# W_out scaled and split early, both parts kept in DRAM, and brought into x^T's place by transfers alone

## The chip, the cores and the metric

The kernel runs on one core of one Trainium2 chip. A core has TensorE (PE, with its weight loads shown as PEld), VectorE (DVE), ScalarE (ACT), GpSimd (POOL) and SyncE (SP), which issues all transfers of this kernel. The metric is the device time of one execution in microseconds (us); a kernel's time is the median over its runs. A profile shows one execution.

## The reference

One layer of a streaming encoder, for 1024 prompt tokens and 64 sample tokens with a past of 512, width 1024. All is fp32.

```python
q_f, k_f, v_f, log_f, u_g, v_g, q_s, k_s, v_s = in_proj(x, w_in, b_f)
o_f = fox attention, 6 heads of 64: softmax(q k^T / 8 + c_t - c_s), c = cumsum(log_f), causal
o_s = stick-breaking attention, 6 heads of 64: sigmoid(z_ts) * prod_{s<j<t} (1 - sigmoid(z_tj))
o_g = gelu(u_g) * (tril(W_s) layer_norm(gelu(v_g)) + b_s)   in chunks of 128, 4 groups of 64
o   = per-head rms_norm(concat(o_f, o_g, o_s)) * g_mix
x   = layer_norm(ALPHA * x + o @ w_out)
x   = layer_norm(ALPHA * x + square(relu(x @ w_up)) @ w_down)
```

The outputs are x for both groups of tokens and the new rows of k, v, log_f and of the normalised v of the gating group.

## The kernel before

**Products.** Every fp32 operand of a matmul is split into a high part and a low part (the rest), and a product is three matmuls: high by high, high by low, low by high. So a weight is loaded, copied to the high part on ACT (L331 and others), and the low part is a subtraction on DVE or POOL (helper `lo_sub`, L97).

**Tokens.** There are nine token tiles: eight of 128 prompt tokens and one of 64 sample tokens. `xT` (L301) holds x transposed, two tiles for the upper and lower 512 rows, each with the high and the low parts of all tokens.

**The first stage** is two streams that the program interleaves by hand (the loop from L1077). `fill()` (L931) makes the projections: for each of six head pairs (three fox, then three stick-breaking) k and v for the nine token tiles, three steps for each tile (`kv_stage`), and q in four parts of three steps (`q_stage`); then the gating v (`sgu_v`) behind the fifth pair, the gating u (`sgu_u`) last, and the first two tiles of the mixing (`mix`, MIXED = 2). `attn()` (L979) makes the attention: for every pair, blocks of 256 queries and two heads (`Unit`), then the sample (`Sample`). The loop takes a step of `attn` when its planned cost is behind that of `fill`; `n_f` counts the steps of `fill`. A new block of queries waits until its q is projected and six further steps of `fill` have passed. The order in which instructions then stand on each engine is made by a scheduler that lists them by a planned time; `in_order` (L100) pins a group of them to the order in which they are written.

A stick-breaking block goes from the scores on PE to the mask on DVE (L561), two sigmoids on ACT (L536, L537), a scan on DVE (L538), a product on POOL (L540), transposes on PE (L602), the split on ACT and DVE (L570, L97), and the product with v on PE (L612 to L615).

**W_out.** The rows of W_out are scaled by `g_mix`, and it takes the place of `xT`, since x^T isn't needed once u is projected. `sgu_u` makes two passes over the nine token tiles, first with the upper 512 rows of x^T and then with the lower ones. After a tile of a pass it issues the pieces of W_out that fit in columns already read (`load_wo`, L964): a piece is 128 rows by 512 columns, loaded into a buffer (tags `vp` or `raw`), scaled and rounded to the high part on ACT (L973), and its low part is made on DVE (L974). There are 16 pieces:

```python
due = [(g, 0, t - 4)] if 4 <= t < 8 else [(0, 1, t)] if g == 1 and t < 4 else []
due += [(1, 1, k) for k in range(4)] if g == 1 and t == NB else []
```

**The mixing** (`mix`, L220) takes token tiles in the order `ORD`. `prep` loads the o rows of a tile (L181) and the gating u (L177), multiplies, and normalises per head (L183 to L192); `o_trans` transposes and splits them (L200, L202, L97), and two groups of 24 matmuls (L244), one for each half of the columns, take W_out as the moving operand; a layer norm follows. The second sub-layer comes after this stage; it is not touched.

Of the kernel before, what the change touches and what calls it, by code (L numbers as in the profile page):

```python
# [12 lines left out]
F32 = mybir.dt.float32  # L13
F32R = mybir.dt.float32r
AF = mybir.ActivationFunctionType
ALU = mybir.AluOpType
# [4 lines left out]
P = 128  # L21
PASSES = ((0, 0), (0, 1), (1, 0))
D = 1024
KT = D // P
# [3 lines left out]
NB = TP // P  # L28
# [28 lines left out]
def _build(nc, tc, a, es):  # L57
# [5 lines left out]
    dr = es.enter_context(tc.tile_pool(name="dr", bufs=1, space=DRAM))  # L63
# [27 lines left out]
    h4_dr = dr.tile([NP, 2, P, 4, 2 * P], F32, name="h4_dr")  # L91
    h3_dr = dr.tile([NP, 2, P, 3, 2 * P], F32, name="h3_dr")
    hs_dr = dr.tile([NP, P, 4, 32], F32, name="hs_dr")
    c_dr = dr.tile([6, TP + PAST + TS], F32, name="c_dr")

    def lo_sub(eng, out, src, hi):
# [2 lines left out]
    @contextmanager  # L99
    def in_order(prev=None):  # L100

        traced = nc.cur_bb.bb.instructions
        last = traced[-1]
        yield
        at = next(k for k in reversed(range(len(traced))) if traced[k] is last) + 1
        prev = {} if prev is None else prev
        for i in traced[at:]:
            p = prev.get(i.engine)
            if p is not None:
                tc.add_manual_dep(i, p.name, mybir.DependencyInfo(  # L110
                    mybir.DependencyClass.NoSync, mybir.DependencyReason.DATA), reason="in_order")
            prev[i.engine] = i

    def dma_r(out, in_):
        nc.sync.dma_start(out.bitcast(F32), in_.bitcast(F32))
# [4 lines left out]
    wo = []  # L120
# [147 lines left out]

    MIXED = 2
    written = set()  # L270
    WOC = 0.5

    def ready(t):
        return ("sb2", min(t // 2, 4)) in written
# [8 lines left out]
    with ExitStack() as p1:  # L283
# [484 lines left out]
            return w  # L768

        def sgu_v(wv):  # L770
            wst = sa.tile([P, 4, 2, P], F32R, name="wst")
            wsr = sp.tile([P, 4, P], F32, name="wsr", tag="row", bufs=ROWS)
            nc.sync.dma_start(wsr, a["w_s"].rearrange("l g i j -> i (l g) j"))
            for g in range(4):
# [39 lines left out]
            for t in range(NT):  # L814
                n = trows(t)
                q = t % 4
# [22 lines left out]

        def sgu_u(wu):  # L840
            part = {}
            nc.sync.dma_start(gmx, a["g_mix"].rearrange("l (k p) -> p (l k)", p=P))
            wo.extend([x[:, :, 0:TP], x[:, :, LO:LO + TP]] for x in xT)
            for g in range(2):
                for t in range(NT):
                    n = trows(t)
                    acc = ps.tile([P, 512], F32, name=f"sgu{t}_{g}", tag="acc", bufs=2)
                    yield from tok_mm(acc, 0, wu, t, 0, 256, range(4 * g, 4 * g + 4))
                    if g == 0:
                        if t % 2 == 0:  # L850
                            part[t // 2] = sa.tile([P, 512], F32, name=f"up{t}", tag="kp", bufs=10)
                        r = part[t // 2][:, (t % 2) * 256:(t % 2) * 256 + 256]
                        nc.scalar.activation(r[0:n], acc[0:n, 0:256], AF.Copy)
                    else:
                        r = part[t // 2][:, (t % 2) * 256:(t % 2) * 256 + 256]
                        nc.vector.tensor_tensor(r[0:n], r[0:n], acc[0:n, 0:256], op=ALU.add)
                    if t == NB:
                        fold(nc.vector, r[0:n], acc, 0, 256)
                    if g == 1:
                        u = sp.tile([P, 256], F32, name=f"sguu{t}", tag="gl", bufs=3)  # L860
                        gelu(u[0:n], r[0:n], n, 256, f"u{t}", nc.gpsimd)
                        nc.sync.dma_start(u_dr[t * P:t * P + n, :], u[0:n])
                        if t == 4:
                            mix_open()
                            preps(2, sa)
                    due = [(g, 0, t - 4)] if 4 <= t < 8 else [(0, 1, t)] if g == 1 and t < 4 else []
                    due += [(1, 1, k) for k in range(4)] if g == 1 and t == NB else []
                    for x in due:
                        load_wo(*x)
                    yield 0.109 * 8  # L870

        pairs = []
# [88 lines left out]
            while live["kp"] > 4:  # L961
                yield None

        def load_wo(i, half, q):  # L964

            k = 4 * i + q
            cs = slice(half * 512, (half + 1) * 512)
            raw = (sa.tile([P, 512], F32, name=f"rwo{k}_{half}", tag="vp", bufs=10) if (2 * k + half) % 3
                   else sp.tile([P, 512], F32, name=f"rwo{k}_{half}", tag="raw", bufs=2))
            nc.sync.dma_start(raw, w_out[:, k, cs])  # L970
            hi = wo[i][0][:, q, cs]
            g = gmx[:, k:k + 1]
            nc.scalar.activation(hi, raw, AF.Copy, scale=g)  # L973
            nc.vector.scalar_tensor_tensor(wo[i][1][:, q, cs], raw, g, hi.bitcast(F32),  # L974
                                           op0=ALU.mult, op1=ALU.subtract)

        cur = {"j": 0}

# [84 lines left out]
            xrs[t] = x_load(t)  # L1063
        load_q(pairs[0])
        x_next = [5, 6, 7, 8]
        F, A = fill(), attn()
        next(A)
        cost = {"f": 0.0, "a": 0.0, "f0": None}
# [8 lines left out]
        while f_live or a_live:  # L1077
            if a_live and pend is None:
                go_a = not f_live or (cost["f0"] is not None
                                      and cost["a"] <= cost["f"] - cost["f0"])  # L1080
            elif a_live:
                if pend in done:
                    lead += 1
                go_a = pend in done and (lead > LEAD or not f_live)
            else:
                go_a = False
            if force_a:
                go_a, force_a = True, False
            if go_a:
                if pend is not None:  # L1090
                    if cost["f0"] is None or pend[1] == 0:
                        cost["f0"], cost["a"] = cost["f"], 0.0
                    pend = None
                    lead = 0
                try:
                    c = next(A)
                    if isinstance(c, tuple):
                        pend = c
                        lead = LEAD if c in seen else 0
                        seen.add(c)  # L1100
                    else:
                        cost["a"] += c * RATIO[cur["j"]]
                except StopIteration:
                    a_live = False
            elif f_live:
                try:
                    c = next(F)
                    if c is None:
                        assert a_live and (pend is None or pend in done), "stuck"
                        force_a = True  # L1110
                        continue
                    cost["f"] += c
                    n_f += 1
                    if x_next and n_f % 3 == 0:
                        xrs[x_next[0]] = x_load(x_next[0])
                        x_next.pop(0)
                except StopIteration:
                    f_live = False
                    while later:
                        flush()  # L1120
# [987 lines left out]
```

## Time and profile before

| | us |
|---|---|
| median of 3 runs | 1408.93 |
| lowest and highest run | 1406.53, 1409.12 |
| the profiled execution, time | 1403.64 |
| the profiled execution, span from first to last instruction | 1401.8 |
| mean granted clock of PE | 0.984 |

The profiled execution is not one of the three runs: its own time lies 5.3 us below their median. The span is what the rows below divide; a granted clock of 1 is the full clock of PE.

### The profile page before, as it was taken

What the parts mean: (1) busy time and instruction counts of PE and PEld (TensorE: products, weight loads), DVE (VectorE), ACT (ScalarE), POOL (GpSimd) and SP (SyncE); (2) the same over time, 40 slices, a digit from 0 to 9 for tenths busy, and PEclk for the clock granted to TensorE, in tenths of its full rate; (3) what the DMA queues carried; (4) which work ended last, traced back from release to release, by engine and by line L of the source; (5) the groups of instructions that cost most, each with busy time, mean ns of one, the idle gap of its engine ahead of it and who ended that gap; (6) DMA issues with size and microseconds to landing.
All of it is one profiled execution on the core that took longest, in us unless ns stands there. A gap on an engine that the chain in (4) does not pass through costs nothing.

```text
span 1401.8 us, 24289 instructions
## 1 busy us (share of the span) xinstructions
PE 1323.6 (94%) x8827; PEld 1205.5 (86%) x8827; DVE 996.3 (71%) x1795; ACT 720.1 (51%) x1561; POOL 608.5 (43%) x667
## 2 busy tenths in 40 slices
PE   7899999999989997999899999999998999999996
PEld 6899999999888986866789999999986788887874
DVE  3566566677787499787776677687668677667677
ACT  3366565666565476333432332322256677667665
POOL 3222232356565445755421222122156765555647
PEclk9999999999999998999999999999999999999998
DMA  7334242321313434432223444443468244344343
GB/s 219 72 84 113 58 113 66 83 59 49 95 27 80 115 97 130 143 112 68 76 85 113 160 152 131 153 141 127 162 223 316 90 169 138 130 153 146 106 135 128
DMA packets 150257, 168.87 MB, mean 120 GB/s; under 512 B 27116, under 2 KB 116524, under 8 KB 150136
## 3 DMA queue, kind: packets, MB, share of 16 engines
q1 hardware_dynamic: 150136, 167.30, 38.1%
q8 instruction: 70, 1.15, 0.3%
q14 instruction: 51, 0.42, 0.1%
HBM read 109.26 MB, written 51.71 MB: 115 GB/s over the span
## 4 chain that ended last, share of the span: by engine, by line
PE 54%; DVE 13%; DMA 10%; POOL 8%; ACT 8%; issue 5%; SPq 1%; DVEq 0%; ACTq 0%; POOLq 0%
PE zA L1272 9%; PE zD L1272 6%; PE mx L244 5%; PE kvsb L355 5%; PE kvfox L355 4%; POOL wd L97 3%; DMA rd<-w_down 3%; PE zC L1272 3%; PE zB L1272 3%; DMA awa<-h_dr 2%; POOL rd L1404 2%; PE qfox L496 2%; PE Sfox L554 2%; ACT wd L1212 2%; PE ptfox L602 1%
## 5 line engine op out<-in xcount | busy, mean ns | idle before, releaser
L97 POOL TENSOR_TENSOR wa<-wr,wa 128x512 fp32r<-128x512 f32 x42 | 63.6, 1544 | 225.3 <-ACT wa L1212 203.8
L97 POOL TENSOR_TENSOR wd<-rd,wd 128x512 fp32r<-128x512 f32 x77 | 100.5, 1317 | 108.0 <-ACT wd L1212 94.8
L244 PE MATMUL mx<-xT,oTb 128*128 128x512 f32 (+1 forms) x416 | 105.6, 405 | 1.6 <-ACT oTb L202 1.5
L1272 PE MATMUL zD<-xo,ws 128*128 128x288 f32 (+1 forms) x720 | 98.1, 289 | 3.1 <-DVE h4a L1436 2.7
L1272 PE MATMUL zA<-xo,ws 128*128 128x288 f32 (+1 forms) x720 | 98.2, 290 | 0.0
L1272 PEld LDWEIGHTS zD<-xo,ws 128*128 128x128 f32 x720 | 93.7, 189 | 3.6 <-DVE h4a L1436 2.9
L244 PEld LDWEIGHTS mx<-xT,oTb 128*128 128x128 f32 (+1 forms) x416 | 76.3, 189 | 21.1 <-ACT oTb L202 2.5
L1272 PEld LDWEIGHTS zA<-xo,ws 128*128 128x128 f32 x720 | 94.3, 190 | 0.0
L355 PE MATMUL kvfox<-wkvfox,xT 128*128 128x256 f32 (+3 forms) x624 | 90.8, 294 | 2.4 <-DVE fx L458 1.3
L540 POOL TENSOR_TENSOR sgsb<-sgsb,snsb 128x127 f32<-128x127 f32 (+7 forms) x48 | 58.9, 1228 | 78.7 <-DVE snsb L538 64.3
L1404 POOL TENSOR_TENSOR rd<-rd 128x512 f32<-128x512 f32 x56 | 79.4, 1419 | 30.4 <-DVE b L97 28.1
L355 PE MATMUL kvsb<-wkvsb,xT 128*128 128x256 f32 (+1 forms) x624 | 87.7, 286 | 0.0
L1212 ACT ACTIVATE wd<-rd 128x512 fp32r<-128x512 f32 x105 | 63.4, 623 | 44.2 <-POOL rd L1404 21.9
L1730 PE MATMUL A<-wd,wd 128*128 128x512 f32 x312 | 83.3, 396 | 3.0 <-DVE acc L1697 2.0
L355 PEld LDWEIGHTS kvfox<-wkvfox,xT 128*128 128x128 f32 (+1 forms) x624 | 81.9, 194 | 4.1 <-DVE fx L458 1.6
L538 DVE TENSOR_TENSOR_SCAN snsb<-snsb,one 128x128 f32<-128x128 f32 (+7 forms) x48 | 72.3, 1509 | 13.3 <-ACT snsb L537 12.7
L355 PEld LDWEIGHTS kvsb<-wkvsb,xT 128*128 128x128 f32 (+1 forms) x624 | 79.3, 187 | 0.2
L1283 ACT ACTIVATE sn<-zA 128x256 f32<-128x256 f32 (+1 forms) x80 | 31.0, 390 | 92.2 <-PE zA L1272 77.5
L1730 PEld LDWEIGHTS A<-wd,wd 128*128 128x128 f32 x312 | 58.0, 188 | 19.1 <-DVE acc L1697 3.5
L1730 PE MATMUL A<-wd,h4a 128*128 128x512 f32 x240 | 64.2, 393 | 1.2 <-DVE acc L1697 0.7
L1490 ACT ACTIVATE ws<-wr 128x1024 fp32r<-128x1024 f32 x28 | 29.0, 1057 | 56.9 <-DVE wr L1222 56.9
L1730 PEld LDWEIGHTS A<-wd,h4a 128*128 128x128 f32 x240 | 44.8, 188 | 12.3 <-ACT wd L1212 1.1
(548 smaller groups left out, 3750.5 us busy)
## 6 DMA issues: line engine op xcount, KB each, us to landing
h_dr<-hh SPq DMA_DIRECT2D x30, 512.0 KB, 3.2
rd<-w_down SPq DMA_DIRECT2D x30, 512.0 KB, 4.4
wr<-w_up SPq DMA_DIRECT2D x13, 1024.0 KB, 5.5
hr<-h_dr SPq DMA_DIRECT2D x31, 384.0 KB, 3.8
h_dr<-hh SPq DMA_DIRECT2D x30, 384.0 KB, 4.0
raw<-w_in SPq DMA_DIRECT2D x44, 256.0 KB, 3.4
hx<-h_dr SPq DMA_DIRECT2D x15, 512.0 KB, 3.8
awa<-h_dr SPq DMA_DIRECT2D x15, 512.0 KB, 4.1
```

The source lines that it names most:

```text
L97: eng.tensor_tensor(out, src, hi.bitcast(F32), op=ALU.subtract)
L244: nc.tensor.matmul(acc[0:m], oT[:, k, hx, 0:m], wo[k // 4][hw][:, k % 4, cs], start=(i == 0), stop=(i == len(seq) - 1))
L355: nc.tensor.matmul(acc[0:n, c0:c0 + n1 - n0], xT[k // 4][:, k % 4, c:c + n], wt[:, k, hw, n0:n1], start=(i == 0), stop=(i == len(seq) - 1))
L496: nc.tensor.matmul(acc[:, 0:w], wq[:, k, hw, :], xT[k // 4][:, k % 4, c:c + w], start=(i == 0), stop=(i == len(seq) - 1))
L538: nc.vector.tensor_tensor_scan(g[:, 0:n][:, ::-1], g[:, 0:n][:, ::-1], one.broadcast_to([P, n]), 1.0, op0=ALU.mult, op1=ALU.bypass)
L540: nc.gpsimd.tensor_tensor(s[:, 0:n - 1], s[:, 0:n - 1], g[:, 1:n], op=ALU.mult)
L1212: nc.scalar.activation(hi, raw, AF.Copy)
L1272: nc.tensor.matmul(z, w[:, hw, k], xop(s, bo, hx)[:, k, :], start=(new and k == 0 and j == 0), stop=(k == 3 and j == 2), skip_group_check= ...
L1283: nc.scalar.activation(c, z, AF.Copy)
L1404: eng.tensor_tensor(r[:, o], r[:, x], r[:, y], op=ALU.subtract)
L1490: nc.scalar.activation(ws[:, 0, q, c], src[:, q], AF.Copy)
L1730: nc.tensor.matmul(z, h[:, hx, q, o], wset[self.c % 2][q][:, hw, wb], start=((n in (0, 3) or n == 1 and self.c == 0) and q == 0 and j == 0 ...
```

## The change

W_out is scaled and split while the fox pairs run. `scale_wo` is a generator of three steps for each of the 16 pieces: load the piece, scale and split it on ACT and DVE, and store both parts into `wo_dr` in DRAM. The loop takes a step of it on every second step of `fill`, from the 32nd on. Its instructions are put behind all those that are already written on their engines (`behind`). Its buffers are two that were there, shared by tag: `sq` of the mixing's squares, and `wst` of the gating weights. In `sgu_u`, `load_wo` now issues only transfers, two of 1 MB (high and low part) at each of four places: after token tiles 3 and 8 of either pass. The load of `g_mix` moves from `sgu_u` to the start of `scale_wo`.

```diff
+    wo_dr = dr.tile([2, 2, 2, P, 4, 512], F32, name="wo_dr")
...
+    def behind():
+
+        return in_order({i.engine: i for i in nc.cur_bb.bb.instructions})
...
-    WOC = 0.5
+    WO_FROM, WO_EVERY = 30, 2
...
-            wst = sa.tile([P, 4, 2, P], F32R, name="wst")
+            wst = sa.tile([P, 4, 2, P], F32R, name="wst", tag="wst", bufs=1)
...
-            nc.sync.dma_start(gmx, a["g_mix"].rearrange("l (k p) -> p (l k)", p=P))
...
-                    due = [(g, 0, t - 4)] if 4 <= t < 8 else [(0, 1, t)] if g == 1 and t < 4 else []
-                    due += [(1, 1, k) for k in range(4)] if g == 1 and t == NB else []
-                    for x in due:
-                        load_wo(*x)
+                    if t in (3, NB):
+                        load_wo(g, t // NB)
...
-        def load_wo(i, half, q):
-
-            k = 4 * i + q
-            cs = slice(half * 512, (half + 1) * 512)
-            raw = (sa.tile([P, 512], F32, name=f"rwo{k}_{half}", tag="vp", bufs=10) if (2 * k + half) % 3
-                   else sp.tile([P, 512], F32, name=f"rwo{k}_{half}", tag="raw", bufs=2))
-            nc.sync.dma_start(raw, w_out[:, k, cs])
-            hi = wo[i][0][:, q, cs]
-            g = gmx[:, k:k + 1]
-            nc.scalar.activation(hi, raw, AF.Copy, scale=g)
-            nc.vector.scalar_tensor_tensor(wo[i][1][:, q, cs], raw, g, hi.bitcast(F32),
-                                           op0=ALU.mult, op1=ALU.subtract)
+        def scale_wo():
+
+            nc.sync.dma_start(gmx, a["g_mix"].rearrange("l (k p) -> p (l k)", p=P))
+            for k in range(KT):
+                for half in range(2):
+                    raw = sa.tile([P, 512], F32, name=f"rwo{k}_{half}", tag="sq", bufs=1)
+                    nc.sync.dma_start(raw, w_out[:, k, half * 512:(half + 1) * 512])
+                    yield
+                    r = sa.tile([P, 4, 2, P], F32R, name=f"swo{k}_{half}", tag="wst", bufs=1)
+                    hi, lo = r[:, 0:2], r[:, 2:4]
+                    g = gmx[:, k:k + 1]
+                    hi, lo = (y.rearrange("p a b c -> p (a b c)") for y in (hi, lo))
+                    nc.scalar.activation(hi, raw, AF.Copy, scale=g)
+                    nc.vector.scalar_tensor_tensor(lo, raw, g, hi.bitcast(F32), op0=ALU.mult, op1=ALU.subtract)
+                    yield
+                    for h, y in enumerate((hi, lo)):
+                        nc.sync.dma_start(wo_dr[k // 4, half, h, :, k % 4], y.bitcast(F32))
+                    yield
+
+        def load_wo(i, half):
+
+            for h in range(2):
+                dma_r(wo[i][h][:, :, half * 512:(half + 1) * 512], wo_dr[i, half, h])
...
+        wo_steps = scale_wo()
...
                     if x_next and n_f % 3 == 0:
                         xrs[x_next[0]] = x_load(x_next[0])
                         x_next.pop(0)
+                    elif n_f > WO_FROM and n_f % WO_EVERY == 0:
+                        with behind():
+                            next(wo_steps, None)
```

## Rows read from the trace of the kernel before

**Rows 1.** The page's first section: busy us (share of the span) xinstructions of each engine.

```profile
PE 1323.6 (94%) x8827; PEld 1205.5 (86%) x8827; DVE 996.3 (71%) x1795; ACT 720.1 (51%) x1561; POOL 608.5 (43%) x667
```

**Rows 2.** Stretches of 20 us: length, busy us of PE, PEld, DVE, ACT, POOL, PEclk, DMA, GB/s.

```profile
120.00:140.00 20.00, 19.34 (x156) 18.11 (x155) 16.52 (x50) 14.08 (x39) 1.29 (x1) 1.00 0.52 138
...
380.00:400.00 20.00, 18.14 (x143) 17.91 (x143) 16.51 (x31) 9.76 (x27) 13.35 (x16) 0.93 0.03 7
...
520.00:540.00 20.00, 17.93 (x138) 17.58 (x137) 18.94 (x29) 14.68 (x34) 8.57 (x7) 0.91 0.23 73
540.00:560.00 20.00, 13.27 (x76) 11.49 (x74) 19.01 (x29) 11.64 (x28) 12.55 (x12) 0.83 0.49 153
...
1060.00:1080.00 20.00, 16.84 (x69) 12.17 (x67) 16.23 (x25) 14.02 (x29) 14.72 (x14) 1.00 0.97 330
```

**Rows 3.** Three longer stretches, with the same columns.

```profile
486.00:543.30 57.30, 51.16 (x408) 49.64 (x408) 53.53 (x77) 44.02 (x106) 23.55 (x22) 0.97 0.37 114
543.30:559.10 15.80, 9.10 (x45) 7.60 (x44) 14.81 (x25) 8.12 (x20) 10.64 (x11) 0.78 0.49 158
...
52.00:240.00 188.00, 181.20 (x1476) 176.06 (x1476) 120.35 (x343) 106.76 (x274) 46.11 (x88) 0.99 0.35 90
```

**Rows 4.** Chain of waits, 486 to 560 us by line, and three of its pieces.

```profile
by line: PE sgu L355 23.5%; issue 15.8%; DVE xT L974 8.9%; PE Ssb L554 7.8%; PE ptsb L602 7.1%; DVE g1u L752 3.9%; DVE pthsb L97 3.4%; PE osb L614 3.2%; PE osb L615 2.8%; DVE snsb L538 2.4%; PE osb L612 2.2%; DVE up L856 2.2%; DVE kc_sb L97
...
528.50 0.26 DVE xT L974
528.75 2.05 issue
530.80 0.74 DVE xT L974
```

**Rows 5.** PE's waits, 484 to 560 us: total us, times, longest us.

```profile
PE Ss0sb L692 <- DVE kc_sb L97: 3.7, 1, 3.7
PE osb L614 <- DVE pthsb L97: 3.4, 3, 1.7
```

**Rows 6.** The tile of W_out's pieces: count, ns min/median/max, first and last start.

```profile
L970 SPq DMA_DIRECT2D rwo<-w_out x16: 327/330/537, 474.1 to 532.4; - x16
L973 ACT ACTIVATE xT<-rwo,gmx x16: 707/733/761, 500.1 to 541.6; 128x512 fp32r<-128x512 f32 x16
L974 DVE SCALAR_TENSOR_TENSOR xT<-rwo,gmx,xT x16: 721/740/2461, 500.9 to 547.7; 128x512 fp32r<-128x512 f32 x16
```

**Rows 7.** Line L974 alone, 486 to 560 us: length, DVE busy, clock, DMA.

```profile
486.00:560.00 74.00, 15.55 (x16) 0.93 0.39 122
```

**Rows 8.** Timeline of DVE and of POOL near 528 us: start, us, engine, line.

```profile
528.41 3.12 DVE L974 SCALAR_TENSOR_TENSOR xT<-rwo,gmx,xT 128x512 fp32r<-128x512 f32 x2
...
528.33 2.00 POOL L540 TENSOR_TENSOR sgsb<-sgsb,snsb 128x1023 f32<-128x1023 f32 x1 [3.24 <-DVE snsb L538]
```

**Rows 9.** The page's DMA issues: count, KB each, median us to landing.

```profile
wr<-w_up SPq DMA_DIRECT2D x13, 1024.0 KB, 5.5
```

**Rows 10.** Timeline of PE: the last sgu matmuls, the first mixing matmuls.

```profile
542.07 1.33 PE L355 MATMUL sgu<-wu,xT 128*128 128x256 f32 x9
...
559.13 6.05 PE L244 MATMUL mx<-xT,oTb 128*128 128x512 f32 x24 [0.24 <-ACT oTb L202]
...
566.31 1.19 PE L244 MATMUL mx<-xT,oTb 128*128 128x512 f32 x4 [0.36 <-ACT oTb L202]
```

**Rows 11.** The tile xT: fox q and stick-breaking k and v, columns as in rows 6.

```profile
L355 PE MATMUL kvsb<-wkvsb,xT x624: 274/281/386, 219.2 to 477.3; 128*128 128x256 f32 x147, 128*64 128x256 f32 x9
...
L496 PE MATMUL qfox<-xT,wqfox x288: 276/281/423, 49.4 to 219.1; 128*128 128x256 f32 x123, 128*128 128x384 f32 x12, 128*128 128x320 f32 x9
```

**Rows 12.** PE's waits, 44 to 240 us: first and last of six rows.

```profile
PE Sfox L554 <- DVE qdfox L505: 3.2, 1, 3.2
...
PE Sfox L554 <- DMA qdfox<-qdfox: 0.2, 1, 0.2
```

**Rows 13.** Timeline of SP: three of the four loads of the first mixing rows.

```profile
540.59 1.39 SPq L181 DMA_DIRECT2D oo<-o_dr  x3
```

## The prediction

> **What bounds the kernel now.** I read the page's first section, then the table of stretches, then the chain of waits of the stage that the change empties, then the waits and stretches of the stage that it fills. The page says that PE is busy for 94% of the span [rows 1], so time can be saved only where PE waits. Two such places belong to this change. The reader is to see them side by side in the table [rows 2]: in 120 to 140 us, a stretch of the fox pairs, PE is busy 19.34 of 20 us though DVE is busy 16.52; in 540 to 560, where u is projected and W_out is split into x^T's place, PE is busy 13.27 and DVE 19.01.
>
> I call the second one the u stage: it goes from 486 us to the first mixing matmul at 559.1. There PE is idle 57.30 - 51.16 = 6.1 us before the last sgu matmul and 15.80 - 9.10 = 6.7 us behind it, 12.8 in 73.1 us; DVE works 53.53 + 14.81 = 68.3 of them [rows 3]. Part of it also runs at the 1.2 GHz level: the granted clock is 0.91 in 520 to 540 and 0.83 in 540 to 560 [rows 2]. The chain of waits of 486 to 560 lies on DVE's L974, the second half of a W_out split, for 8.9% of 74 us, 6.6 us, more than on any other line of DVE, and a further piece of 2.05 us, called issue, stands between two L974 pieces [rows 4]. Among PE's own waits the two longest are on DVE results that stood behind these splits: 3.7 us for kc_sb and 3.4 for pthsb [rows 5]. So in the u stage DVE is the limit and W_out's splits are a part of its load.
>
> **What is removed from the u stage.** Sixteen loads of 256 KB, sixteen ACT copies of 0.733 us and sixteen DVE operations of 0.740 us median [rows 6]. On ACT that is 11.7 us, on DVE 11.8 us by the median; by the table DVE spent 15.55 us on them [rows 7], because some ran long: one pair took 3.12 us from 528.41, while POOL's multiply of 2.00 us began at 528.33 [rows 8]. What is saved I read in two ways. By the chain: 6.6 + 2.05 = 8.6 us. By a like stretch: 380 to 400 has a stick-breaking pair beside projection and no splits of W_out; DVE is busy 16.51 of 20 there and PE 18.14, a share of 0.907 [rows 2]. Without the splits DVE has 68.3 - 15.6 = 52.8 us left in the u stage, and PE 51.16 + 9.10 = 60.3. At a share of 0.907 that takes 60.3 / 0.907 = 66.4 us, with DVE at 80%, much as in the like stretch. That saves 73.1 - 66.4 = 6.7 us. I take the mean of the two, **7.7 us**. Bounds: 12.8 us if PE never waits (a little more with the clock up), and 0 if something else is late next. What is late next is the rest of the chain: PE's remaining sgu and attention matmuls, and the o rows that are normalised before the first mixing tile.
>
> The Trainium skill has a rule for the long pair ("SBUF — State Buffer", section "SBUF: two separate sides"): a VectorE operation with two SBUF inputs and a GpSimd operation that reads SBUF lock each other out for a whole instruction. This trace agrees in the 3.12 us pair. By the rule part of the 15.55 - 11.8 = 3.7 us isn't removed, since POOL's multiplies would then hold up the next scan or split instead; the sum would be some 2 us less than one that counts all of it. It also says that the sixteen operations meet POOL in the fox pairs, but POOL works 46.11 of 188 us there, against 23.55 + 10.64 = 34.2 of 73.1 in the u stage [rows 3], so they would meet it half as often.
>
> **What is added to the u stage.** Eight transfers of 1 MB from DRAM, two at each of four places. A transfer of this size lands 5.5 us after its issue [rows 9]. Each pair may start only when PE has read the columns that it overwrites. The last pair, for the second half of columns of the lower rows, waits for token tile 7 of the second pass; the last sgu matmuls run at 542.07, and the half is first needed by the second 24 mixing matmuls, at 566.31 [rows 10]. Two transfers one behind the other take at most 11 us of these 24, and the other three pairs have more. Costed at nothing; the cover is the first half of the first mixing tile (6.05 us) and the attention work before it. If that cover were gone, up to 11 us would be seen.
>
> **What is added to the fox pairs.** The same sixteen ACT and DVE operations, the sixteen loads, and thirty-two stores of 256 KB. One step is taken on every second fill step from the 32nd on, three steps a piece, so pieces end near fill step 126. The first pair's 27 projection steps end as its q projection starts, at 49.4; the 117th step ends near 219.2, where the first stick-breaking pair's projection starts [rows 11]. That is 170 us for 90 steps, 1.9 us a step, 11 us a piece, and the work lies between some 53 and 236 us. PE is busy 181.20 of 188 us there, DVE 120.35, ACT 106.76 [rows 3]: 68 us of DVE's time and 81 of ACT's are free for 11.8 and 11.7. The cover is thus idle time between DVE's and ACT's own operations, and what is paid is the delay of an operation that comes just behind a piece, where PE waits for that one. PE's waits for other engines sum to 6.6 us over 44 to 240, in six rows, from 3.2 us for qdfox down to 0.2 [rows 12]. With DVE's load up by 11.8 / 120.35 = 10% and ACT's by 11%, these grow by 0.65 us in proportion; queues grow faster than the load, so I double it: **1.3 us**. Bounds: nothing, and the whole 11.8 us of DVE if each piece delays PE for its full length. I stay near the low end because the stretch with DVE at 16.52 of 20 [rows 2], fuller than the 14.1 of 20 that the pieces make of the mean, cost PE only 0.66 us.
>
> On SP, a load waits for the piece before it (4 steps, 7 us, earlier) and a store for DVE's split (2 steps earlier). Behind a late store stand k and v rows, q copies and weight loads. A DVE operation late by a microsecond holds these back by as much; by the written order six fill steps pass between a q projection and the first use of its copies. I count nothing beyond the 1.3 us. The traffic is 12 MB more over 183 us, 4 MB read and 8 MB written, 69 GB/s on top of 90 in a stretch where the DMA share is 0.35 [rows 3]. Each piece's buffers were there before and are free in this stage: they cost nothing. The load of the gains moves with the rest and is one small transfer.
>
> **Sum.** -7.7 + 1.3 = -6.4 us. The profiled execution took 1403.64 us, with its span 1401.8; that gives 1397.2 for such an execution. It lies 5.3 us under the median of the runs, 1408.93, so I put the change against that: 1408.93 - 6.4 = **1402.5 us**.
>
> **The rivals.**
> *The forecast* (DVE relieved, cost hidden): 0.68. Its own range is a saving of 11.5 to 2.5, 1397.4 to 1406.4.
>
> *Another chain takes over in the u stage.* PE lost 1.86 of 20 us in 380 to 400 with no split in it [rows 2]: the round from scores to sigmoid, scan, multiply and transposes could set the pace, with POOL's multiply behind each scan. Then 0 to 2 us are saved and 1.3 paid: 1408 to 1410. Against it stands that L974 itself is on the chain. 0.13.
>
> *The big transfers hold up the small ones.* The mixing starts with o rows that were loaded by three DMAs issued from 540.59 on [rows 13], the very time at which the last pair of 1 MB goes out. At the 330 GB/s that a full stretch reached [rows 2], 2.1 MB take 6.4 us. If the o rows wait for these, 7.7 - 6.4 - 1.3 leaves nothing: 1409, or some 2 us worse if copies of the attention wait as well. For it: one queue serves both. Against: three of these loads were issued 18.5 us before the first mixing matmul [rows 10, 13], so that a delay of 6.4 us may be hidden as well. 0.10. The Trainium skill speaks for this rival ("DMA: Bandwidth & Descriptors", section "Queues, rings and completion order"): on each DMA engine the descriptors of one queue are consumed in ring order. No row here shows a small load that is held up by a large one.
>
> *Slower: the fox pairs pay in full.* PE is busy all of 188 us but 6.8 there, so a late operand can't be made up. If each moved DVE operation sits in front of an operand that PE needs next, PE loses 16 times 0.74 = 11.8 us against 7.7 saved: +4.1, 1413. It decides from 7.7 / 11.8 = 65% of the moved DVE time on. Against it stands the full stretch with only 0.66 us lost. 0.09.
>
> **How the numbers follow.** 0.2% is 2.8 us, about what a measurement of this kernel can tell from no change: faster means under 1406.1, slower over 1411.7. Faster: 0.65 of the forecast's 0.68, 0.03 of the second case, 0.03 of the third: 0.71. Same: 0.03, 0.08 and 0.05: 0.16. Slower: 0.09, 0.02 and 0.02: 0.13. The range starts at a saving of 13.5 (12.8 and a little clock), 1395.4, and leaves the slower cases out above 1409.5.
>
> **What would show it.** In the profile after: L974's like among the fox pairs, 16 times near 0.74 us, with PE's share between 53 and 236 us down by no more than some 1.5 us in all; in the u stage DVE's share at 80 to 85% instead of 93, no split on the chain, PE's waits for kc_sb and pthsb mostly gone, the granted clock nearer 1.0, the first mixing matmul some 6 us earlier, and no wait of a mixing matmul for a transfer. It is wrong if that matmul isn't earlier (another chain, or the o rows behind the big transfers), or if it is late already by 240 us (the fox pairs pay).

## The result, and the profile after

The kernel after takes 1408.97 us (median of 20 runs), the kernel before 1404.99 in the 20 runs beside them; the ratio is 1.0031 with a 95% interval of 1.0019 to 1.0043. So it is slower, by about 4 us (2.7 to 6.0), where 6.4 us less were forecast. (The three runs of before that the forecast started from had a median of 1408.93; the 20 go from 1398.26 to 1409.12.) The time lies inside the range by half a microsecond, but by luck: the three runs stood 3.9 us above the median of the 20, and from that median the range would have ended at 1405.6. The sign is wrong. The profiled execution took 1411.56 us, its span 1409.7, against 1403.64 and 1401.8 before.

First the stage that the change empties. The lines of the tile x^T in the profile after (count, ns min/median/max, first and last start) answer to [rows 6, 10, 11]:

```profile
L501 PE MATMUL qfox<-xT,wqfox x288: 276/281/419, 49.9 to 222.9; 128*128 128x256 f32 x123, 128*128 128x384 f32 x12, 128*128 128x320 f32 x9
...
L360 PE MATMUL sgu<-wu,xT x208: 274/282/387, 495.7 to 550.9; 128*128 128x256 f32 x98, 128*64 128x256 f32 x6
...
L249 PE MATMUL mx<-xT,oTb x416: 388/394/776, 560.2 to 685.8; 128*128 128x512 f32 x134, 128*64 128x512 f32 x5
...
L120 SPq DMA_DIRECT2D xT<-wo_dr x8: 524/531/597, 510.0 to 552.3; - x8
```

The trace of before has, for the second and the third line,

```profile
L355 PE MATMUL sgu<-wu,xT x208: 275/282/415, 486.3 to 543.1; 128*128 128x256 f32 x98, 128*64 128x256 f32 x6
...
L244 PE MATMUL mx<-xT,oTb x416: 388/394/772, 559.1 to 682.9; 128*128 128x512 f32 x134, 128*64 128x512 f32 x5
```

The reader is to take three distances from them. From the first sgu matmul to the first mixing matmul it is 560.2 - 495.7 = 64.5 us, against 559.1 - 486.3 = 72.8 before: the u stage is 8.3 us shorter. From the first q projection of the fox pairs to the first sgu matmul it is 495.7 - 49.9 = 445.8 us against 486.3 - 49.4 = 436.9: 8.9 us longer, before the u stage begins. And the mixing takes 125.6 us from its first to its last start against 123.8. By the first mixing matmul the kernel after is 1.1 us behind.

Stretches of 20 us, columns as in [rows 2], which they answer to but for the last:

```profile
120.00:140.00 20.00, 19.03 (x154) 17.88 (x154) 16.29 (x50) 14.96 (x37) 2.59 (x3) 1.00 0.60 159
380.00:400.00 20.00, 17.31 (x121) 16.87 (x122) 14.21 (x30) 10.73 (x30) 10.62 (x20) 0.83 0.18 48
...
520.00:540.00 20.00, 19.75 (x167) 19.47 (x165) 15.22 (x23) 13.56 (x33) 9.88 (x7) 1.00 0.59 205
540.00:560.00 20.00, 14.71 (x97) 12.58 (x96) 19.31 (x32) 11.78 (x27) 12.86 (x13) 0.92 0.81 269
720.00:740.00 20.00, 11.36 (x70) 11.13 (x69) 6.72 (x17) 2.79 (x6) 2.35 (x2) 0.74 0.46 147
```

In 520 to 540, DVE fell from 18.94 to 15.22 us, PE rose from 17.93 to 19.75, and the clock from 0.91 to 1.00. The last row is new: in 720 to 740, where the second sub-layer has just begun, PE is busy 11.36 of 20 us, and in the kernel before 17.86:

```profile
720.00:740.00 20.00, 17.86 (x127) 17.45 (x126) 9.54 (x18) 3.67 (x8) 4.87 (x3) 0.91 0.62 190
```

The timeline of after there, first PE, then ACT, then SP's queue (start, us; in brackets the idle time and what ended it):

```profile
729.33 2.05 PE L1289 MATMUL zA<-xo,ws 128*128 128x288 f32 x7 [8.64 <-ACT sn L1300]
...
728.87 0.41 ACT L1300 ACTIVATE sn<-zA 128x288 f32<-128x288 f32 x1 [11.31 <-DMA h_dr<-y]
...
725.61 0.38 SPq L1335 DMA_DIRECT2D h_dr<-y  x1
```

and the same ACT instruction in the kernel before:

```profile
717.08 0.41 ACT L1283 ACTIVATE sn<-zA 128x288 f32<-128x288 f32 x1 [1.60 <-PE zA L1272]
```

PE waits 8.64 us for an ACT instruction that itself waits 11.31 us, not for PE's product, as it did before, but for a store to DRAM, h_dr<-y. Nothing in the diff touches this part of the kernel, and from here to the end the order of instructions is the same in both.

What differs is an address. The seven rotating buffers `row` of 4 KB per partition are handed out in the order in which the scheduler of the build places the tiles that use them. The pieces of W_out changed that order upstream, and with it which row of the second sub-layer's first part (y0 to y8) lies where. When that part ends, the space is given to a new pool, `lp`, whose eight tiles lie one behind the other in a written order of tags. The first instruction that writes such a tile waits for the last user of the same addresses. The addresses in the two built programs (bytes in a partition):

```
tile of lp     before and after     row buffer under it     its last rows: before    after
sn0            103104 to 105408     101120 to 105216        y4, then y2              y1, then y7
```

(sn0 is the tag of the tile that the lines call sn. The next weight load, `wr`, lies at 83648 to 91840 in both; the rows under it are y0, y5 and y6 before, and y0, y3 and y6 after.)

y7's rows end as those in which half of a chain's h is kept until it is stored; y3's hold the other half. y2's rows hold a weight at that time, which DVE reads for the last time up to 715.79 us in the trace of before, 1.3 us ahead of sn's write at 717.08. So in the kernel after sn's first write now stands behind the last store of the stage before it.

### The profile page after: what moved, and what is told of

It reads as the page before. It is cut to its first block, busy times and chain, and to the rows that moved or that the text cites. A ratio compares the mean times of both kernels' runs of the same rounds, so it can differ in the third digit from the quotient of the medians.

```text
span 1409.7 us, 24345 instructions
## 1 busy us (share of the span) xinstructions
PE 1326.3 (94%) x8827; PEld 1205.3 (85%) x8827; DVE 999.0 (71%) x1795; ACT 721.6 (51%) x1561; POOL 607.7 (43%) x667
## 4 chain that ended last, share of the span: by engine, by line
PE 69%; DVE 12%; DMA 6%; POOL 4%; issue 4%; ACT 4%; SPq 1%; DVEq 0%; ACTq 0%; POOLq 0%
PE A L1747 10%; PE zA L1289 10%; PE zD L1289 6%; PE kvsb L360 5%; PE mx L249 5%; PE D L1747 5%; PE kvfox L360 4%; PE zC L1289 3%; PE zB L1289 3%; PE B L1747 2%; PE qsb L501 2%; PE Sfox L559 1%; PE ptfox L607 1%; DMA xr<-x_prompt 1%; PE ds L1793 1%
## 5 line engine op out<-in xcount | busy, mean ns | idle before, releaser
L1747 PE MATMUL A<-wd,h4a 128*128 128x512 f32 x240 | 64.4, 394 | 0.9 <-DVE acc L1714 0.7
L1714 DVE TENSOR_TENSOR acc<-acc,A 128x512 f32<-128x512 f32 x73 | 49.2, 680 | 8.8 <-PE A L1747 8.7
```

Source lines behind the costliest of these rows:

```text
L1714: nc.vector.tensor_tensor(out, out if other is None else other, bank, op=ALU.add)
L1747: nc.tensor.matmul(z, h[:, hx, q, o], wset[self.c % 2][q][:, hw, wb], start=((n in (0, 3) or n == 1 and self.c == 0) and q == 0 and j == 0 ...
```

## The experiments

Each line is a kernel; the time of before beside it was taken together with it on the same chip. The last two columns are from its profile: first fox q projection to first sgu matmul, and the u stage.

| kernel | median us | before | ratio, 95% interval | q fox to sgu | u stage |
|---|---|---|---|---|---|
| before | | | | 436.9 | 72.8 |
| after | 1408.97 | 1404.99 | 1.0031, 1.0019 to 1.0043 | 445.8 | 64.5 |
| after_relaid | 1400.37 | 1403.29 | 0.9976, 0.9966 to 0.9987 | 442.4 | 64.4 |
| before_aliased | 1409.94 | 1403.29 | 1.0046, 1.0028 to 1.0063 | 434.9 | 72.9 |
| u_only | 1393.17 | 1403.29 | 0.9920, 0.9905 to 0.9934 | 439.5 | 64.3 |
| fox_only | 1407.35 | 1403.29 | 1.0024, 1.0011 to 1.0037 | 438.3 | 72.9 |
| u_spread | 1396.20 | 1403.18 | 0.9950, 0.9936 to 0.9964 | 436.8 | 64.2 |
| late_split | 1398.30 | 1403.18 | 0.9971, 0.9956 to 0.9986 | 442.8 | 64.2 |
| no_stores | 1408.78 | 1403.18 | 1.0039, 1.0023 to 1.0054 | 450.6 | 64.6 |
| late_fill | 1416.32 | 1403.18 | 1.0098, 1.0079 to 1.0118 | 461.8 | 66.6 |
| late_start | 1400.95 | 1403.12 | 0.9980, 0.9967 to 0.9993 | 445.0 | 64.2 |
| start_50 | 1396.16 | 1403.12 | 0.9946, 0.9929 to 0.9963 | 441.4 | 64.2 |
| cb_behind | 1404.79 | 1403.12 | 1.0004, 0.9985 to 1.0024 | 451.9 | 64.3 |
| tight_50 | 1403.75 | 1403.22 | 1.0005, 0.9989 to 1.0021 | 444.3 | 64.5 |

A single profile scatters: after, after_relaid and fox_only have the same order of instructions up to the u stage, and their "q fox to sgu" goes from 438.3 to 445.8. In after, 1.4 of the 8.9 us against before were lost by 68 us, and the first piece's load was issued at 69.2. So verdicts on the fox pairs go by the ratios. In every kernel but after and before_aliased the two tiles of `lp` that are written first, sn0 and wr, lie clear of late rows (y3 and y7), by themselves in before and late_start, by another order of the tags in the others.

**The address, both ways.** The change with only the order of the tags altered:

```diff
-        for tag, n in (("wa", 3072), ("wr", 2048), ("hh1", 2048), ("sn1", 768), ("sn0", 768), ("hh0", 2304), ("ws", 4096),
+        for tag, n in (("wr", 2048), ("sn0", 768), ("hh1", 2048), ("sn1", 768), ("wa", 3072), ("hh0", 2304), ("ws", 4096),
```

> The changed kernel with every instruction in the same order; only the order in which the eight buffers of the second sub-layer are laid into the first stage's memory differs, so that the first copy of its second product (sn) and the next weight load no longer lie on the rows of token tiles 3 and 7, which are read last by a store at 725 us. Placement theory: the 8.6 us wait of PE at 720 to 729 in the profile after falls to about 2 us, and the kernel gets 6.5 us shorter than the changed one, about 0.998 of the kernel before. Fox theory (the whole loss lies in the fox pairs, and the wait at 720 is an accident of one execution): it stays near 1.003.

and the kernel before with an order that puts sn0 and wr on y7's rows:

```diff
-        for tag, n in (("wa", 3072), ("wr", 2048), ("hh1", 2048), ("sn1", 768), ("sn0", 768), ("hh0", 2304), ("ws", 4096),
+        for tag, n in (("sn1", 768), ("sn0", 768), ("wr", 2048), ("hh1", 2048), ("wa", 3072), ("hh0", 2304), ("ws", 4096),
```

> The kernel before, every instruction in the same order, with the same eight buffers laid so that sn and the weight load do lie on the rows of token tile 7. Placement theory: a wait of some 8 us appears behind 717 us and the time rises by about 6.5 us, to 1.0045 of before. Fox theory: no change, 1.000.

Measured: 0.9976 and 1.0046. In the second kernel the wait of after has come into the kernel before, at the same instruction and of the same length; ACT's sn, then PE's product behind it:

```profile
725.42 0.41 ACT L1283 ACTIVATE sn<-zA 128x288 f32<-128x288 f32 x1 [11.33 <-DMA h_dr<-y]
...
725.88 3.25 PE L1272 MATMUL zA<-xo,ws 128*128 128x288 f32 x12 [8.66 <-ACT sn L1283]
```

In the first it is gone: the stretch 720 to 740 of after_relaid reads

```profile
720.00:740.00 20.00, 18.47 (x146) 18.06 (x146) 8.75 (x16) 3.65 (x8) 4.88 (x3) 1.00 0.63 190
```

against 11.36 in after. The address costs 0.46% of 1403 us, 6.5 us, by one pair and 0.55%, 7.7 us, between after and after_relaid. It decides the sign: without it the change is faster, by 0.24%. The traces agree: if the same matmuls are matched with those of before, PE falls back by some 7.0 us between 712 and 760 us in after as in before_aliased. In the eleven others, ten of them with other orders of the tags than that of before, the same figure goes from 1.4 gained to 0.4 lost, so the order of the tags does little by itself.

**The two halves of the change.** u_only and u_spread keep the u stage's transfers and drop scaling and splitting altogether. In u_only one store of 1 MB from x^T's place fills what all eight transfers read; in u_spread eight stores fill eight places:

```diff
-                    elif n_f > WO_FROM and n_f % WO_EVERY == 0:
+                    elif 40 <= n_f < 72 and n_f % 4 == 3:
                         with behind():
-                            next(wo_steps, None)
+                            e = (n_f - 40) // 4
+                            nc.sync.dma_start(wo_dr[e // 4, e // 2 % 2, e % 2], xT[0][:, :, 0:512].bitcast(F32))
```

fox_only does the fox pairs' part, and in the u stage still splits W_out as before (`load_wo` and `due` of the kernel before).

> Leaves out the scaling and splitting of W_out: one store of 1 MB from x^T's tile in the first fox pair, and the eight transfers of 1 MB in the u stage all read that place. Buffers laid so that neither sn nor the weight load waits. If the relief of DVE in the u stage is worth what was forecast, 7.7 us are saved: 0.9945 of before. Rival (the 1 MB transfers or another chain take the gain): 0.998 to 1.001.

> Only the u stage's part of the change, as before (no scaling and no split anywhere, output not the reference's), but with eight stores of 1 MB from x^T's place into eight places, and each transfer of the u stage reading its own, where the earlier run read one place eight times. If reading one place again and again was no advantage, 0.992 again; if the four microseconds by which that run and the run of the fox pairs' part did not add up came from there, 0.995.

> W_out is scaled, split and stored among the fox pairs as in the change, but the u stage does its own sixteen pieces as in the kernel before, so the work is done twice. Buffers laid so that neither sn nor the weight load waits. Fox theory: the cost of the fox pairs alone is over 8 us, 1.006 or more. Placement theory: it is what the profile after shows from 60 to 480 us, 4 to 8 us, 1.003 to 1.0055. The forecast's step was 1.3 us, 1.001.

Measured: 0.9920, 0.9950 and 1.0024. The u stage lasts 64.2 to 64.6 us in the eleven kernels that have its transfers, wherever the splits went, but for late_fill (66.6), and 72.8 or 72.9 in the three that split there. From u_spread, the u stage's half is worth 0.50% of 1403 us, 7.0 us (5.1 to 9.0); from fox_only, the fox pairs pay 0.24%, 3.4 us (1.5 to 5.2). Their sum, -3.6 us, is after_relaid's -3.4. With the address, 6.5 to 7.7, it comes to +2.9 to +4.1, about what was measured (the 7.7 is itself taken from after, so that only the 2.9 is independent of it). That u_only is some 4 us faster still than u_spread, with a u stage of the same length, stays open; it has seven stores of 1 MB less. The sum closes only with u_spread: by u_only the half would be worth 11.2 us, and with fox_only's 3.4 the sum would be -7.8.

**What the fox pairs pay for.** The pieces in the profile after, and what their engines waited for just ahead of them:

```profile
L982 SPq DMA_DIRECT2D wo_dr<-swo x32: 319/360/1047, 73.1 to 251.2; - x32
L978 ACT ACTIVATE swo<-rwo,gmx x16: 711/723/728, 72.4 to 248.6; 128x512 fp32r<-128x512 f32 x16
L979 DVE SCALAR_TENSOR_TENSOR swo<-rwo,gmx,swo x16: 736/751/870, 73.1 to 249.4; 128x512 fp32r<-128x512 f32 x16
its engine sat idle before it (us, times) until:
  DMA rwo<-w_out: 15.0, 9
  ACT swo L978: 13.0, 11
```

The operations are as long as forecast, and none runs long beside POOL. But ACT stood idle 15.0 us until a load had landed, and DVE 13.0 us until ACT's copy was there, where the prediction gave these waits no term. So the first theory was that the load is late. One more step between load and split tests it:

```diff
                     nc.sync.dma_start(raw, w_out[:, k, half * 512:(half + 1) * 512])
                     yield
+                    yield
```

> The change, with the early row buffers laid so that no late reader of a row holds up the second sub-layer, and with one more step between the load of a piece and its split (four steps, about 7 us, in place of two), so that the copy on ACT finds its data there. If what the fox pairs pay (3.4 us) comes from ACT standing in wait for each load, most of it goes, and the ratio to before falls from 0.9976 to about 0.9955, with ACT's idle time before these copies near nothing. If the price is that of the work itself, or of the traffic, the ratio stays at 0.9976.

Measured 0.9971 against 0.9976: no difference. ACT's wait for loads fell only from 12.0 us (after_relaid) to 7.4, and the pieces now run on to some 310 us, into the stick-breaking pairs. It neither shows nor excludes the theory. no_stores leaves the thirty-two stores out (`scale_wo` without its last loop; eight stores of 1 MB as in u_spread):

> The change, laid without the late row, with the sixteen loads and splits in the fox pairs but without the thirty-two stores of the parts; eight stores of 1 MB from x^T's place stand for them in fox pair 0, so that the transfers in the u stage have eight places to read (the output isn't the reference's). If the loads and splits carry the price of the fox pairs, the ratio to before is that of the change without the late row, 0.9976; if the stores with their waits on SP's queue and their traffic carry it, the ratio is that of the kernel that has only the u stage's part, 0.992. Halves of each give 0.995.

Measured 1.0039, slower than with the stores. It is inconclusive: the stand-in stores of 1 MB run among the pieces, and with the steps changed the scheduler placed PE's work in another order.

If the same matmuls are matched in two traces and their starts subtracted, the kernels with pieces from step 32 on fall back against before between 70 and 85 us, where the first pair's attention opens; after_relaid goes from 3.4 us ahead to 0.7 behind, and stays near 1 behind through 250. There DVE's first mask operation waits for two transfers that spread the cumulative gates, cbfox<-c_dr; it starts at 72.11 us in after_relaid and at 72.68 in before, so that 0.6 of the 3.4 us are left. Their time to landing (count, KB each, median us), in before, u_spread, after_relaid and after:

```profile
cbfox<-c_dr SPq DMA_DIRECT2D x2, 512.0 KB, 4.6
```

```profile
cbfox<-c_dr SPq DMA_DIRECT2D x2, 512.0 KB, 4.4
```

```profile
cbfox<-c_dr SPq DMA_DIRECT2D x2, 512.0 KB, 6.9
```

```profile
cbfox<-c_dr SPq DMA_DIRECT2D x2, 512.0 KB, 6.3
```

The first piece's load of 256 KB was issued on SP's queue 1.4 to 1.5 us ahead of them. That suggested three runs: late_start and start_50 change one constant, to 60 and to 50 (start_50 and cb_behind reorder the tags, too), and cb_behind adds to late_start a load of 512 KB that nothing reads.

```diff
-    WO_FROM, WO_EVERY = 30, 2
+    WO_FROM, WO_EVERY = 60, 2
...
+                    elif n_f == 36:
+                        with behind():
+                            ahead = sa.tile([P, 4, 2, P], F32R, name="ahead", tag="wst", bufs=1)
+                            nc.sync.dma_start(ahead.rearrange("p a b c -> p (a b c)").bitcast(F32), w_out[:, 0, :])
```

> The change with one constant altered: the pieces start after fill step 60 in place of 30, behind the first fox pair's opening. In the profiles with pieces from step 32 on, the two small transfers cbfox<-c_dr land 6.0 to 6.9 us after their issue, in the kernel before and in the one without pieces 4.4 to 4.6; DVE's first mask operation waits for them, and PE falls back by about 4 us in 70 to 85 us and by nothing later. If that one place is the price of the fox pairs, cbfox lands in 4.4 to 4.6 us again, PE keeps its place through 100 us, and the ratio to before is 0.995 (row buffers fall so that nothing late lies under the second sub-layer's first tiles). If the price is spread over the sixteen pieces, the ratio is about 0.9976, as in the change laid without the late row.

> The same with step 50, and the early tiles of the second sub-layer laid clear of late rows: the first piece's load stands directly behind the first pair's opening. By the one place as the price: 0.995. By a price spread over the pieces: 0.9976.

> Pieces from step 60 as in late_start, and one more load of 512 KB from W_out into a free buffer, which nothing reads, issued between the store of the cumulative gates and the two transfers cbfox<-c_dr (no ACT or DVE work with it). If a transfer on the queue holds up the small ones behind it, cbfox lands some 6.5 us after its issue, PE falls back by 2 to 4 us at 70 to 85 us, and the ratio is that of late_start plus 0.002. If the price came from ACT's and DVE's work or the stores, cbfox lands as in late_start and nothing changes.

Measured: start_50 0.9946, as expected of the one place; late_start 0.9980, not. In both, cbfox landed in 4.4 and 4.6 us and PE kept its place there. But late_start's pieces end at some 310 us, and it goes from 1.2 us ahead at 250 us to 5.3 behind at 300, 4.4 us of it after 290, early in the stick-breaking pairs. The granted clock of 300 to 320 is 0.83 there, and among PE's waits of 180 to 340 us the largest sum is that of three waits on ACT, 2.6 us; the stretch, then the waits:

```profile
300.00:320.00 20.00, 17.98 (x131) 17.54 (x131) 14.47 (x25) 13.77 (x37) 13.51 (x16) 0.83 0.41 126
```

```profile
PE Ssb L559 <- ACT snsb L542: 2.6, 3, 1.4
```

What makes up the rest isn't shown.

In cb_behind, cbfox landed in 6.0 us, as expected of a queue that holds up the small transfers, but PE fell back there by 0.9 us only; its further loss, to a ratio 0.0024 above late_start's, came between 160 and 320 us in its trace, and the two intervals overlap. So the opening is one place at which pieces cost something, about 1 us of it by the queue, and it isn't the whole price. Whether cbfox lands late because it stands behind the load in the queue or because both share the DMA engines, these runs don't tell apart.

Two last kernels put the pieces elsewhere: tight_50 is start_50 with the stores in the step of the next load, so that the pieces are over by 240 us; late_fill sets them beside V's projection and the last pair (step 191 on, one step a fill step, two steps a piece, parts in free k and v tiles), in 384 to 486 us.

```diff
                     nc.scalar.activation(hi, raw, AF.Copy, scale=g)
                     nc.vector.scalar_tensor_tensor(lo, raw, g, hi.bitcast(F32), op0=ALU.mult, op1=ALU.subtract)
                     yield
                     for h, y in enumerate((hi, lo)):
                         nc.sync.dma_start(wo_dr[k // 4, half, h, :, k % 4], y.bitcast(F32))
-                    yield
```

> As start_50 (pieces from step 50 on, early tiles clear of late rows), with a piece in two steps in place of three: its stores stand in the step of the next load, so the sixteen pieces end some 30 fill steps earlier, before the stick-breaking pairs open. If start_50 still pays for the pieces that it has among these (its PE fell back from -2 at 250 us to +2 at 320), 0.993; if the pieces' density counts, so that each delays ACT and DVE more often, 0.996 or above; otherwise 0.9946 again.

> The change, laid without the late row, with the sixteen pieces moved out of the fox pairs: from fill step 191 on, one step a fill step, beside V's projection and the last pair's projections (some 420 to 480 us), where the trace of before shows DVE busy 8.39 and 4.69 of 20 us in 440 to 480; the parts lie in free k and v tiles. If the price is DVE's and ACT's load beside the fox pairs, the ratio is near that of the u stage's part alone, 0.992 to 0.994. If 12 MB in some 60 us hold up the weights and rows of the last pair, or the pieces beside V's normalisation hold up DVE there, 0.998 or more.

Measured: 1.0005 and 1.0098, both worse. Here the first theory is seen at work once. In tight_50, in order of engine ACT, DVE, PE:

```profile
186.28 0.72 ACT L978 ACTIVATE swo<-rwo,gmx 128x512 fp32r<-128x512 f32 x1 [1.57 <-DMA rwo<-w_out]
...
187.04 0.75 DVE L979 SCALAR_TENSOR_TENSOR swo<-rwo,gmx,swo 128x512 fp32r<-128x512 f32 x1 [2.99 <-ACT swo L978]
...
189.23 0.74 PE L559 MATMUL Sfox<-kpfox,qdfox 128*128 128x256 f32 x4 [2.23 <-DVE mfox L531]
```

The load was issued at 182.26; ACT stood for it, DVE, idle for 2.99 us, stood for ACT, the mask operation behind the split came late, and PE waited 2.23 us for it. ACT's wait for loads was 17.6 us in tight_50, 24.7 in late_fill (where PE once waited 10.0 us for kpsb, behind pieces), 12.4 in start_50. The two largest sums are those of these two slow kernels; between 7 and 15 us they don't order the kernels (no_stores has 10.2 and 1.0039, start_50 12.4 and 0.9946). So that the standing idle is what costs is shown for this one wait, and argued for the rest.

What follows: counted from u_spread's 0.9950, sixteen pieces cost between nothing (start_50, 0.9946) and 21 us (late_fill), by place and density, and some 4 us more if counted from u_only's 0.9920; as placed in the change, 3.4 us by fox_only. How these 3.4 divide among load, split, stores and the order that the scheduler chose is not settled. start_50, 7.0 us below before, beats both kernels: 1396.16 us, 0.54% faster than before, where after is 0.31% slower.

## Why the prediction was wrong, point by point

**The u stage: right.** Forecast a saving of 7.7 us; the stage lost 8.3 in the profile, and the half alone is worth 7.0 in the runs (11.2 by u_only, which stays open). PE's waits for kc_sb are gone, those for pthsb are 3.7 us in six pieces against 3.4 in three [rows 5]; in 540 to 560 DVE is still full, with 19.31 of 20, and over the stage its share is 85% (55.11 of 64.50 us). The like stretch (6.7) and the chain (8.6) bounded it from both sides.

**The eight transfers and the o rows: right at the first mixing matmul, with cover left.** No mixing matmul waited for one, though they took 7.5 us to land, not 5.5. The last pair took 11.3 us from its first issue (550.20) to its last landing (561.50), where at most 11 were forecast, and the first matmul of the second half of the columns started at 566.86. The o rows took 6.3 us (median of eight) against 3.4 before:

```profile
xT<-wo_dr SPq DMA_DIRECT2D x8, 1024.0 KB, 7.5
oo<-o_dr SPq DMA_DIRECT2D x8, 256.0 KB, 6.3
```

The rival of big transfers ahead of small ones has its mechanism here, and in cbfox's landing, but not its price: the first of the rows were issued at 539.62, 20.6 us ahead of the first mixing matmul. By the rule of the Trainium skill that stood with that rival ("DMA: Bandwidth & Descriptors", section "Queues, rings and completion order": one queue's descriptors are taken in ring order), the trace agrees, with 6.3 us against 3.4, and with a row load that was issued at 552.86, 0.58 us behind the last transfer of 1 MB, and landed at 562.19, 0.69 us behind it. The mixing itself took 1.8 us longer, which no step foresaw. It lasts 124.3 to 127.1 us in ten of the eleven kernels with the eight transfers (late_fill 123.1) and 123.6 to 123.8 in the three without, so it seems to go with them; what does it isn't settled.

**The fox pairs: mostly hidden, as forecast, but the term too small.** Forecast 1.3 us, measured 3.4 (1.5 to 5.2), far from the 11.8 of the rival that pays in full. PE's busy time between 53 and 236 us fell from 176.20 to 172.20 us in the profile, by 4.0 where the prediction allowed some 1.5. The step "I count nothing beyond the 1.3 us" is the one that was mis-sized. It took the pieces' busy time as load and had no term for an engine in order that stands idle in front of a piece until its load has landed (15.0 us on ACT, 13.0 on DVE), nor for a load that goes ahead of cbfox on the queue. The queue's part is some 1 us by cb_behind; that the idle time makes up the rest is argued, not shown, since late_split cut it and gained nothing that can be told from no change. (By the prediction's own 1.9 us a step the 32nd step stands near 59 us, not 53; nothing hangs on it.)

**The step that failed: "Each piece's buffers were there before and are free in this stage: they cost nothing."** It is true of the pieces' own buffers. But new tiles and new steps change the order in which the scheduler hands out buffers that the diff doesn't name. No term of the sum and no rival stood for that, and its 6.5 to 7.7 us took more than the net gain of 3.4. So of the way from -6.4 to the measured +4, the address is 6.5 to 7.7 us, the fox pairs are 2.1 and the u stage 0.7 (with u_spread). Where it would be seen was not in the list of what to look at either: all of that ends with the mixing.

## What to carry to other kernels

When work is moved in a kernel whose buffers rotate and whose pools share addresses, compare the addresses of the two builds as well as the instructions: a tile that is written first should lie on space that was given back first, and an order of tags is a free way to see to that. Price a moved piece by what stands in order behind its load on each engine and queue at the spot where it lands, not by its busy share; two places that are full alike can differ by several microseconds, so try more than one start. And look for the loss by following the shift of the same matmuls through both traces: here it moved in steps, a loss at 70 to 85, a gain at 500 to 560 and a loss at 720 us, and the largest loss lay where the diff changes nothing.

## What the runs showed that was not expected

An operation that waits for an address shows in the trace as an engine that waits for a store: ACT's 11.31 us "<-DMA h_dr<-y" has no data in common with it. And PE's idle 8.64 us are not what it cost. The granted clock of 720 to 740 is 0.74 in after and 1.00 in after_relaid, so part of that stretch ran at the 1.2 GHz level: behind the 8.66 us in which PE stood idle in before_aliased, the twelve matmuls zA<-xo,ws took 3.25 us (the line shown for that kernel), and in the kernel before, where PE came to them without a pause,

```profile
718.47 1.75 PE L1272 MATMUL zA<-xo,ws 128*128 128x288 f32 x12
```

By the matched matmuls PE is 11.2 us further behind by 722 us, in after as in before_aliased, and then wins 4.2 us back by 737, where the kernel before has waits and a lower clock of its own (0.91 in 720 to 740). What is left is some 7.0 us; the runs put it at 6.5 to 7.7.
